# A two-layer trunk on one core: input loads moved in the queue, maxima taken one by one inside blocks, fewer gate products kept for the end, and output weights loaded before they are split

## The chip, the cores and the metric

The kernel runs on one core of a Trainium2 chip. The metric is the device time of one execution in microseconds (us). A core has five engines, each with an instruction stream of its own, that meet over semaphores: TensorE (PE in the profile; PEld is its weight load), VectorE (DVE), ScalarE (ACT), GpSimd (POOL) and SyncE (SP), which here only issues DMAs.

## The reference

The sequence has 2048 tokens, the model width is 1024, all in float32, and the result has to keep float32 accuracy. Layer 0 is forgetting attention with 16 heads of 64; layer 1 is sliding-window attention (window 128) with 16 query heads over 4 shared heads, and learned sinks.

```
u = rmsnorm(x, norm_a_g);  q, k, v, f, gate = split(u @ w_in_a)
q, k = rmsnorm per head(q), rmsnorm per head(k)
c = cumsum(log_sigmoid(f + b_forget))                      # per head, over the tokens
p = softmax(q.k / 8 + c[query] - c[key], causal);  o = p @ v
h = x + (o * silu(gate)) @ w_out_a
k_s, v_s = split(rmsnorm(h, kv_norm_g) @ w_kv)             # 4 heads; k normed, rotated
q, gate = split(rmsnorm(h, norm_b_g) @ w_in_b)             # 16 heads; q normed, rotated
o = softmax over the last 128 keys and the head's sink (q.k / 8) @ v_s
out = h + (o * silu(gate)) @ w_out_b
```

## The kernel before, in words

Every float32 product of the projections is made as three products of split operands: a tile is cast to a rounded half (the names with h: `uh`, `wh`) and a remainder (`ul`, `wl`), and uh·wh, uh·wl and ul·wh are summed. So a block of 128 tokens by 512 columns over the depth of 1024 (8 slices of 128, index `dt`) is 24 matmuls, at L571.

The stages follow each other in this order.

1. **Projections of layer A** (`projections`). Seven groups of columns (v of heads 0 to 7, two of k, three of q, the middle one of which waits for the forget logits of the one ahead of it, then v of heads 8 to 15), each over 16 token blocks `tb`. In the first group the token tiles are loaded as they are needed: `norm` loads one x tile of 128x1024 (L298), ACT squares it (L300), L286 to L291 make the factor, L304 scales; `norm_transpose` turns it on PE (L277) and splits it (L313 on ACT, L314 on DVE). `normer.upto` keeps two tiles loaded ahead. The small vectors (gains, biases, sinks; `load_vectors`, L212) and the positions (L228) are loaded on the same SP queue; `vectors` and `angles` use them at blocks VECTORS_AT and ANGLES_AT. `weights` loads raw weights (L337, two slices of `dt` in one DMA), and ACT and DVE split them (L350 and L351, with a gain L354 and L355).
2. **The forget gates** (`forget`): the jobs of that function, among them `running` (matmuls at L614 with a triangle and a matrix of ones, DVE at L619 and on) and `rows` (transposes and rows written out), run at the blocks FORGET_AT of the next group.
3. **Maxima ahead.** The attention (`attention_a`) is a generator. In the last v group `hook(tb)` calls it: it starts with `load_max` for head 0 (L680 to L682: ka, ca, qa in forms for the maxima) and then `max_pieces`, one for each 128 queries and up to 1024 keys: matmuls (L738) into a PSUM tile `b2`, and DVE's running maximum (L747, L752). EARLY of them run there; at piece REST_AT `load_rest(0)` loads what the scores of head 0 need (L686, L687, L693). During projections PSUM has three tiles `b2`, which the blocks and the pieces share, and `pa`, `pb`.
4. **Attention A**: 320 steps, each a 128-key-block pair of `scores` (L784, L785; exponent on ACT L793, cast L798, remainder on POOL L799, sums on DVE L810) and `values` (L825, three steps later), with maxima of later heads (`ahead`) and `gate`, a filler that yields one product at a time (768 in all, L855: weights `wr` loaded from `wg` at L851, results stored at L862). `feed((total - KEPT) * (n + 1) // 320)` spreads all products but KEPT over the steps; eight each follow the last three steps. At the steps PREP_AT one pair of heads is finished (`gated_load`, L986 to L991, then `gated`: POOL L1001, DVE L1004 and L1005, ACT L1006, DVE L1007).
5. **The tail of attention A.** The last sums are inverted (`recips`, L709), the rest of the filler runs, and between its products `half` loads and splits the first half of w_out_a (tile `st`), calling `between(k)` after each two slices for the pairs that are left. Then `out_a` loads and splits the second half in the same way (L337, `st`), multiplies (L1045) and adds x.
6. **Layer B**: projections of shared k and v, of q and gate, then `attention_b`, units of 128 tokens and one shared head, with the output projection (L1191) as its filler. At unit B_AHEAD the first half of w_out_b, `W[0]`, is loaded and split (four loads of `wr`, L337; ACT L350, DVE L351).

The order on each engine is set by the framework's scheduler, which takes instructions as they become ready by priority; `keep_in_program_order` pins an instruction behind the one written before it on its engine. Tiles are buffers of named slots that are passed on when their last reader is done: `big` 8, `st` 4, `wr` 2, `wh` and `wl` 9 each, `qn` 3, `sq` 2. All DMAs are issued by SP in one order, and one that waits holds those behind it.

Of the kernel before, what the change touches and what calls it, by code (L numbers as in the profile page):

```python
# [21 lines left out]
P = 128  # L22
# [8 lines left out]
CH = 512  # L31
# [12 lines left out]
PREP_AT = (286, 294, 304, 311)  # L44
# [3 lines left out]
KEPT = 6 * 3 * NDT  # L48

NORM_AHEAD = 2  # L50
QK_LAG = 1
# [4 lines left out]
EARLY = 21  # L56
REST_AT = 8

VECTORS_AT = 11
ANGLES_AT = 9  # L60
FORGET_AT = (1, 3, 5, 6, 7, 8)
# [23 lines left out]
class Trunk:  # L85
# [124 lines left out]
    def load_vectors(self, loads):  # L210
        for t, src in loads:
            self.nc.sync.dma_start(out=t, in_=src, allow_slow_non_contiguous=True)  # L212
# [10 lines left out]
    def angles(self):  # L223

        nc, a = self.nc, self.a
        sh = [P, NTB, 8]
        pi = self.sb("sq", [P, NTB], I32)
        nc.sync.dma_start(  # L228
            out=pi, in_=a["positions"].rearrange("(t p) -> p t", p=P),
            allow_slow_non_contiguous=True,  # L230
        )
# [44 lines left out]
    def flip(self, out, in_):  # L276
        self.nc.tensor.transpose(out, in_, self.ident)  # L277
# [38 lines left out]
    def weights(  # L316
        self, src, c0, w, gain=None, extra=None, into=None, ahead=None, tag="wr", between=None
    ):

# [11 lines left out]
        for dt in range(NDT):  # L331
# [94 lines left out]
    def normer(self, src):  # L426
# [11 lines left out]
        def upto(n, loads=()):  # L438

            loads = list(loads)  # L440
# [12 lines left out]
    def projections(self, normed, groups, later=None, pre=None, hook=None):  # L453
# [8 lines left out]
        if pre is not None:  # L462
# [11 lines left out]
            norm(1, [partial(load_raw, 0), partial(self.load_vectors, self.loads[:1])])  # L474
            for dt in range(2, NDT, 2):
                load_raw(dt)
# [48 lines left out]
        for gi, grp in enumerate(groups):  # L525
# [31 lines left out]
            for tb in range(NTB):  # L557
                norm(tb + NORM_AHEAD)
                if hook is not None and gi == len(groups) - 1:
                    hook(tb)  # L560
# [8 lines left out]
                for dt in range(NDT):  # L569
                    for i, (u, k) in enumerate(((uh, 0), (uh, 1), (ul, 0))):  # L570
# [28 lines left out]
    def forget(self, z):  # L599
# [10 lines left out]
        def running():  # L610
            both = self.ps("b2", [P, 2, NTB, H])
            inb, tot = both[:, 0], both[:, 1]
            for o, m in ((inb, self.tri), (tot, self.ones)):
                nc.tensor.matmul(  # L614
                    o.rearrange("p t h -> p (t h)"), m, flat, start=True, stop=True
# [6 lines left out]
        def rows(ch):  # L622
            sc = -float(HD) ** 0.5
            tr = self.ps(("pa", "pb")[ch % 2], [H, 4, P])
            for j in range(4):
                self.flip(tr[:, j, :], z[:, ch * 4 + j, :])
# [27 lines left out]
    def attention_a(self, w_out, result):  # L654
# [64 lines left out]
        def max_pieces(h, ch):  # L719
# [5 lines left out]
            def piece(j, part):  # L725
# [11 lines left out]
                for b in range(nb):  # L737
                    nc.tensor.matmul(  # L738
# [3 lines left out]
                    )  # L742
                o = m[:, j : j + 1] if parts == 1 else mt[:, j, part : part + 1]
# [154 lines left out]
        def prepare_load():  # L898
# [4 lines left out]
            if k < 5 or k % 2 == 0:  # L903
# [29 lines left out]
        for n, (u, p) in enumerate(steps):  # L933
# [17 lines left out]
            if n == SILU_AT:  # L951
                silus()
            if n in PREP_AT:
# [20 lines left out]
    def half(self, w, i, tag="wr", between=None):  # L974
# [3 lines left out]
            w, i * CH, CH, tag=tag, between=between,  # L978
# [77 lines left out]
    def attention_b(self, w_out, res, dst):  # L1056
# [152 lines left out]
        for n in range(N + V_LAG_B):  # L1209
# [6 lines left out]
            if n == B_AHEAD:  # L1216
                W[0] = self.weights(w_out, 0, CH)
# [18 lines left out]
    def layer_a(self):  # L1236
# [27 lines left out]
        def hook(tb):  # L1264
            if tb >= MAX_AT:
                next(steps)
# [82 lines left out]
```

## Time and profile before

| | before |
|---|---|
| time, median of 3 runs | 2584.24 us (2583.28 to 2587.08) |
| time of the profiled execution | 2575.79 us |
| its span | 2574.1 us, TensorE clock granted 0.991 on average |
| PE busy | 2488.1 us, 97 % |
| DVE, ACT, POOL busy | 1671.7, 1357.1, 939.4 us |
| DMA | 420.34 MB, 163 GB/s on average |

The span runs from the first to the last instruction of the profiled execution, and all positions below are microseconds from its start. A wait is listed with the engine that stood, the instruction that stood (tile, line), and what it waited for. "2.0, 1, 2.0" behind it is the sum, how often, and the longest. A row of the timeline has the start, the length, the engine, line, operation, the tile written and read, and in brackets how long the engine had been idle and for what.

### The profile page before, as it was taken

Reading aid. Unit: us, or ns where it says so; the run is one execution under the profiler, and the core shown is the slowest. Engines: PE = TensorE matmul, PEld = TensorE weight load, DVE = VectorE, ACT = ScalarE, POOL = GpSimd, SP = SyncE. Lnnn points to the kernel's source line nnn. Section 1 sums busy time; section 2 is a strip of 40 time slices with the busy share of each in tenths; the row PEclk is TensorE's granted clock in tenths of the full one; section 3 lists DMA queues with packets and bytes.
Section 4 is the critical chain, followed back from the end, with each engine's and each line's share of the span. In section 5 each row is a group of like instructions: output and inputs, shape, how many; then the busy total and the mean of one; then the engine's idle time right before and its main releaser. Section 6 shows DMA issues by size and latency. Waiting matters only on the chain. (4 is left out here: it accounts for less than half of the span.)

```text
span 2574.1 us, 37683 instructions
## 1 busy us (share of the span) xinstructions
PE 2488.1 (97%) x12414; PEld 2069.8 (80%) x12414; DVE 1671.7 (65%) x4125; ACT 1357.1 (53%) x2645; POOL 939.4 (36%) x611
## 2 busy tenths in 40 slices
PE   7999999989999999999999979999999999899999
PEld 6888899967888777787787758778888888788887
DVE  5455556623888878888888834446756401688885
ACT  5423323312878788787788732224422213777774
POOL 0000000010878777888778822200011000355552
PEclk9999999999999999999999999999999999999999
DMA  5556555676654665566554678964434513756642
GB/s 165 172 171 177 163 149 163 188 216 197 169 151 121 189 168 184 149 179 187 135 145 136 175 224 246 272 207 140 138 96 115 152 70 117 207 147 170 172 140 66
DMA packets 357298, 420.34 MB, mean 163 GB/s; under 512 B 65104, under 2 KB 248400, under 8 KB 350928
## 3 DMA queue, kind: packets, MB, share of 16 engines
q1 hardware_dynamic: 357104, 417.94, 56.1%
q8 instruction: 98, 1.61, 0.3%
q14 instruction: 96, 0.79, 0.1%
HBM read 264.23 MB, written 153.49 MB: 162 GB/s over the span
## 5 line engine op out<-in xcount | busy, mean ns | idle before, releaser
L571 PE MATMUL b<-wh,big 128*128 128x512 f32 (+3 forms) x2560 | 771.7, 376 | 11.1 <-DVE mt L747 4.3
L799 POOL TENSOR_TENSOR big<-st,big 128x1024 fp32r<-128x1024 f32 (+1 forms) x320 | 678.7, 2134 | 255.5 <-ACT big L798 199.3
L571 PEld LDWEIGHTS b<-wh,big 128*128 128x128 f32 x2560 | 472.6, 189 | 85.2 <-DVE mt L747 6.3
L571 PE MATMUL b<-wl,big 128*128 128x512 f32 (+3 forms) x1280 | 474.4, 371 | 0.3 <-DVE wl L355 0.3
L810 DVE TENSOR_TENSOR ac<-ac,st 128x512 f32<-128x512 f32 (+3 forms) x576 | 355.4, 617 | 60.9 <-ACT st L793 32.3
L825 PE MATMUL pa<-big 128*128 128x512 f32 (+2 forms) x1280 | 329.3, 372 | 1.6 <-POOL big L799 0.8
L793 ACT ACTIVATE st<-sc 128x512 f32<-128x512 f32 (+1 forms) x512 | 274.3, 585 | 100.5 <-PE sc L785 61.7
L798 ACT CAST big<-st 128x1024 fp32r<-128x1024 f32 (+1 forms) x320 | 302.6, 946 | 7.8
L571 PEld LDWEIGHTS b<-wl,big 128*128 128x128 f32 x1280 | 242.3, 189 | 36.0 <-DVE wl L355 2.6
L825 PEld LDWEIGHTS pa<-big 128*128 128x128 f32 x1280 | 224.8, 190 | 41.8 <-ACT sq L833 6.4
L784 PE MATMUL sc<-big 128*128 128x512 f32 (+2 forms) x640 | 245.9, 384 | 3.0 <-ACT st L793 3.0
L367 ACT ACTIVATE sq<-b 128x512 f32<-128x512 f32 (+2 forms) x128 | 66.2, 517 | 339.5 <-PE b L571 339.4
L747 DVE CUSTOM_DVE_ANT_0 mx<-mx,rot 128x960 f32<-128x960 f32 (+3 forms) x242 | 213.1, 880 | 47.5 <-PE mx L738 43.9
L785 PE MATMUL sc<-big 67*128 67x512 f32 (+2 forms) x640 | 235.7, 368 | 0.0
L855 PE MATMUL pb<-wh,wr 128*128 128x512 f32 x512 | 189.9, 407 | 19.5 <-DMA wr<-wg 18.4
L738 PE MATMUL mx<-big 66*128 66x320 f32 (+2 forms) x666 | 194.9, 365 | 5.2 <-DVE mt L752 2.9
L369 DVE TENSOR_REDUCE sm<-sq 128x8 f32<-128x512 f32 (+2 forms) x128 | 74.9, 585 | 172.0 <-ACT sq L367 171.8
L1045 PE MATMUL b<-big 128*128 128x512 f32 x768 | 178.6, 393 | 5.6 <-DVE qn L1049 4.3
L1045 PEld LDWEIGHTS b<-big 128*128 128x128 f32 x768 | 144.8, 190 | 38.5 <-DVE qn L1049 5.7
L542 PE MATMUL b<-big,wh 128*128 128x512 f32 x512 | 158.6, 391 | 0.9 <-ACT st L548 0.9
L664 POOL MEMSET rot<- 128x1024 bf16 x1 | 1.0, 951 | 428.7 <-PE pb L277 428.7
L1126 POOL TENSOR_TENSOR st<-st,rs 128x1024 f32<-128x1024 f32 (+1 forms) x64 | 118.5, 1852 | 98.8 <-DVE rs L1125 89.7
(212 smaller groups left out, 4193.5 us busy)
## 6 DMA issues: line engine op xcount, KB each, us to landing
wr<-wg SPq DMA_DIRECT2D x64, 512.0 KB
va<-st SPq DMA_DIRECT2D x32, 512.0 KB
ka<-st SPq DMA_DIRECT2D x64, 256.0 KB
ut<-big SPq DMA_DIRECT2D x16, 1024.0 KB
big<-ka SPq DMA_DIRECT2D x16, 1024.0 KB
big<-qa SPq DMA_DIRECT2D x16, 1024.0 KB
qb<-st SPq DMA_DIRECT2D x64, 256.0 KB
big<-qb SPq DMA_DIRECT2D x16, 1024.0 KB
```

Of the source, the lines that this page charges most:

```text
L571: nc.tensor.matmul(ps[:, :n], u[tb // 4][:, dt, us], W[k][dt], start=(dt == 0 and i == 0), stop=(dt == NDT - 1 and i == 2),)
L738: nc.tensor.matmul(ps[:, b, :wb], qb[:66, i * P : (i + 1) * P], kb[:66, k0 + b * wb : k0 + (b + 1) * wb], start=True, stop=True,)
L747: nc.vector.tensor_tensor_reduce(out=lg, in0=lg, in1=mask, scale=1.0, scalar=NEG, op0=ALU.add, op1=ALU.max, accum_out=f_(o),)
L784: nc.tensor.matmul(o, ka[:, ks], qa[:, qs], start=not (last and n_), stop=False)
L785: nc.tensor.matmul(o, kb[:, ks], qb[:, qs], start=False, stop=not diag)
L793: nc.scalar.activation(pf[:, off : off + w], ps[:, :w], AF.Exp, scale=HD**-0.5)
L798: nc.scalar.copy(ph[:, :tw], pf[:, :tw])
L799: nc.gpsimd.tensor_tensor(pl[:, :tw], pf[:, :tw], f_(ph[:, :tw]), ALU.subtract)
L810: nc.vector.tensor_tensor(a_, a_, pf[:, off : off + w], ALU.add)
L825: nc.tensor.matmul(pv[:, q0 : q0 + w], v[:, k, :], src[:, off : off + w], start=(p == 0 and n_ == 0 and i == 0), stop=(last and n_ == 1 an ...
L855: nc.tensor.matmul(ps, w[:, dt // 2 % 2, wk, dt % 2, :], us[dt][uk], start=(dt == 0 and i == 0), stop=(dt == NDT - 1 and i == 2),)
L1045: nc.tensor.matmul(ps, y[p // 4][:, k, p % 4, ts_], W[nh][j][p], start=(p == 0 and i == 0), stop=(p == NDT - 1 and i == 2),)
```

## The change: eight edits

- **Start.** The loads of the vectors and of the positions are pinned in program order, VECTORS_AT goes from 11 to 8 and ANGLES_AT from 9 to 11, `upto` loads three tiles ahead, and the raw weights of the first group are asked for behind x tile 1 in one piece.
- **Forget gates.** FORGET_AT is spread to later blocks, and the matmuls of `running` and the transposes of `rows` are pinned.
- **Maxima.** `hook` is called for every `dt`: `load_max` stays at block 5, and from block 8 on one piece goes behind the products of dt 0, 3 and 5 of each block, in place of two pieces at the start of each block from 5 on. EARLY is 24 (all of head 0) in place of 21, REST_AT 3 in place of 8, and the pieces' matmuls are pinned.
- **Gate products.** KEPT is 96 in place of 144.
- **Output weights of layer A.** At step 302 the raw first half of w_out_a is loaded in four DMAs into one `big` tile; `half` splits them from that tile. The second half is loaded through `st` as before.
- **Pairs.** PREP_AT has five steps in place of four, so a fifth pair of heads is finished within the steps; the tiles of pair 5 and 7 are `qn`, `wh`, `wl` in place of `st`.
- **`between`** feeds in every call.
- **Output weights of layer B.** `W[0]` is made in four parts, at units 6 to 9, two slices each.

```diff
-PREP_AT = (286, 294, 304, 311)
+PREP_AT = (284, 293, 304, 309, 314)
+RAW_AT = 302
-KEPT = 6 * 3 * NDT
+KEPT = 4 * 3 * NDT
+LOADED_AHEAD = 3
-EARLY = 21
-REST_AT = 8
-VECTORS_AT = 11
-ANGLES_AT = 9
-FORGET_AT = (1, 3, 5, 6, 7, 8)
+EARLY = 24
+REST_AT = 3
+VECTORS_AT = 8
+ANGLES_AT = 11
+FORGET_AT = (1, 5, 8, 9, 10, 11)
...
 def load_vectors(self, loads):
     for t, src in loads:
-        self.nc.sync.dma_start(out=t, in_=src, allow_slow_non_contiguous=True)
+        self.tc.keep_in_program_order(
+            self.nc.sync.dma_start(out=t, in_=src, allow_slow_non_contiguous=True)
+        )
...
 def weights(self, src, c0, w, ..., between=None,
+    dts=range(NDT),
...
-        for dt in range(NDT):
+        for dt in dts:
...
 def upto(n, loads=()):
-                while done[0] < min(done[1] + 2, NTB):
+                while done[0] < min(done[1] + LOADED_AHEAD, NTB):
                     ready.append(self.norm(src, done[0], junk))
                     done[0] += 1
-                    if loads:
-                        loads.pop(0)()
+                    if done[0] > 1:
+                        for load in loads:
+                            load()
+                        loads = ()
...
             for tb in range(NTB):
                 norm(tb + NORM_AHEAD)
-                if hook is not None and gi == len(groups) - 1:
-                    hook(tb)
...
                 for dt in range(NDT):
+                    if hook is not None and gi == len(groups) - 1:
+                        hook(tb, dt)
                     for i, (u, k) in enumerate(((uh, 0), (uh, 1), (ul, 0))):
...
-        yield
         for n in range(EARLY):
+            yield
             if n == REST_AT:
                 load_rest(0)
             ahead(n + 1)
-            yield
+        yield
...
-            if k < 5 or k % 2 == 0:
+            if k != 6:
                 tiles = [self.sb(t, [P, CH]) for t in ("qn", "wh", "qn", "wl")]
...
             feed((total - KEPT) * (n + 1) // len(steps))
+            if n == RAW_AT:
+                raw = self.sb("big", [P, NDT, CH])
+                for dt in range(0, NDT, 2):
+                    nc.sync.dma_start(out=raw[:, dt : dt + 2, :], in_=w_out[...])
...
         def between(k):
-            prepare()
-            if k < 3:
+            if prepared < NDT:
+                prepare()
+            if len(ready) < NDT:
                 prepare_load()
-                feed(fed + (total - fed) // (4 - k))
+            feed(fed + (total - fed) // (4 - k))
-        result.append(self.half(w_out, 0, "st", between))
+        result.append(self.half(w_out, 0, ahead=raw, between=between))
...
-            if n == B_AHEAD:
-                W[0] = self.weights(w_out, 0, CH)
+            if B_AHEAD <= n < B_AHEAD + NDT // 2:
+                hs, ls = self.weights(w_out, 0, CH, dts=(2 * (n - B_AHEAD), 2 * (n - B_AHEAD) + 1))
+                W[0] = [W[0][0] + hs, W[0][1] + ls] if W[0] else [hs, ls]
...
-        def hook(tb):
-            if tb >= MAX_AT:
-                next(steps)
+        def hook(tb, dt):
+            if (tb, dt) == (MAX_AT, 0) or tb >= MAX_AT + 3 and dt in (1, 4, 6):
                 next(steps)
```

The order of SP at the start, before. `st<-in_x` and `wr<-in_x` are the token tiles, `big<-in_w_in_a` the first weights, the short tiles the small vectors:

```order
L467 DMA big<-in_w_in_a 128x2x512 x4
L298 DMA st<-in_x 128x1024
L298 DMA wr<-in_x 128x1024 x2
L228 DMA sq<-in_positions 128x16x1
L212 DMA bf<-in_b_forget 128x16
L212 DMA g_qa<-in_qnorm_a_g 64x1 x2
L212 DMA g_ka<-in_knorm_a_g 64x1 x2
L212 DMA g_b<-in_norm_b_g 128x8x1
L212 DMA g_kv<-in_kv_norm_g 128x8x1
L414 DMA va<-st 128x8x128
L212 DMA g_qb<-in_qnorm_b_g 64x1 x2
```

The same place after:

```order
L478 DMA big<-in_w_in_a 128x2x512 x4
L306 DMA st<-in_x 128x1024
L306 DMA wr<-in_x 128x1024 x2
L306 DMA st<-in_x 128x1024
L424 DMA va<-st 128x8x128
L306 DMA wr<-in_x 128x1024
L424 DMA va<-st 128x8x128
L306 DMA st<-in_x 128x1024
L424 DMA va<-st 128x8x128
```

The positions and the vectors stood ahead of the x tile of block 4 and the first store of v; now the x tiles go on, the vectors come between the va stores of blocks 5 to 7 (five and nine of them, behind the x tiles of blocks 9 and 10), and the positions behind the store of block 10.

PE at the first maxima, in the last v group, before (L571 is the block, L738 a piece; the number tells the PSUM tile):

```order
L571 MATMUL b_5245<-wh,big 128x512
L738 MATMUL b_5290<-big 128x128
L571 MATMUL b_5293<-wh,big 128x512
...
L571 MATMUL b_5293<-wh,big 128x512
L738 MATMUL b_5322<-big 128x256
L738 MATMUL b_5325<-big 128x384
L571 MATMUL b_5329<-wh,big 128x512
```

And after, where a block is at L584 and a piece at L753:

```order
L753 MATMUL b_5382<-big 128x128
L584 MATMUL b_5377<-wh,big 128x512
...
L584 MATMUL b_5377<-wh,big 128x512
L753 MATMUL b_5394<-big 128x256
L584 MATMUL b_5377<-wh,big 128x512
...
L584 MATMUL b_5377<-wh,big 128x512
L753 MATMUL b_5403<-big 128x384
L584 MATMUL b_5377<-wh,big 128x512
```

Two pieces between two blocks became one piece each between products of one block, and the first piece comes three blocks later.

SP behind the last store of inverted sums (`rd`), before. `wr<-wg` are weights of the filler, `gt` its results, `om`, `oc`, `rd` what a pair needs:

```order
L715 DMA rd<-sq 48x32
L851 DMA wr<-wg 128x1024 x2
L862 DMA gt<-sq 128x512
L337 DMA st<-in_w_out_a 128x2x512 x2
L986 DMA st<-om 128x512
L987 DMA st<-oc 128x512
L851 DMA wr<-wg 128x1024
L988 DMA st<-gt 128x512
L851 DMA wr<-wg 128x1024
L862 DMA gt<-sq 128x512
L991 DMA st<-rd 64x512 x2
```

After:

```order
L730 DMA rd<-sq 48x32
L1013 DMA qn<-gt 128x512
L879 DMA gt<-sq 128x512
L347 DMA st<-in_w_out_a 128x2x512
L868 DMA wr<-wg 128x1024
L347 DMA st<-in_w_out_a 128x2x512
L868 DMA wr<-wg 128x1024
L879 DMA gt<-sq 128x512
L347 DMA st<-in_w_out_a 128x2x512
L868 DMA wr<-wg 128x1024
```

Until the pairs that come last are loaded, four weights of the filler and four pairs of slices of w_out_a (the second half) are behind that store now, where there were ten and seven (of both halves).

More of the change, by code (lines that the diff above doesn't have):

```diff
@@ L276, in flip @@
     def flip(self, out, in_):
-        self.nc.tensor.transpose(out, in_, self.ident)
+        return self.nc.tensor.transpose(out, in_, self.ident)
     def rstd(self, sm, n, count):
@@ L316, in weights @@
     def weights(
-        self, src, c0, w, gain=None, extra=None, into=None, ahead=None, tag="wr", between=None
+        self, src, c0, w, gain=None, extra=None, into=None, ahead=None, tag="wr", between=None,
+        dts=range(NDT),
     ):
@@ L472, in load_raw @@
                 )
-            norm(1, [partial(load_raw, 0), partial(self.load_vectors, self.loads[:1])])
-            for dt in range(2, NDT, 2):
-                load_raw(dt)
+            norm(
+                1,
+                [partial(self.load_vectors, self.loads[:1])]
+                + [partial(load_raw, dt) for dt in range(0, NDT, 2)],
+            )
         else:
@@ L613, in running @@
             for o, m in ((inb, self.tri), (tot, self.ones)):
-                nc.tensor.matmul(
-                    o.rearrange("p t h -> p (t h)"), m, flat, start=True, stop=True
+                self.tc.keep_in_program_order(
+                    nc.tensor.matmul(
+                        o.rearrange("p t h -> p (t h)"), m, flat, start=True, stop=True
+                    )
                 )
@@ L737, in piece @@
                 for b in range(nb):
[L738 removed]
+                    mm = nc.tensor.matmul(
                         ps[:, b, :wb], qb[:66, i * P : (i + 1) * P],
@@ L742, in piece @@
                     )
+                    if "mx" not in self.banks:
+                        self.tc.keep_in_program_order(mm)
                 o = m[:, j : j + 1] if parts == 1 else mt[:, j, part : part + 1]
@@ L952, in attention_a @@
                 silus()
+            if n == RAW_AT:
+                raw = self.sb("big", [P, NDT, CH])
+                for dt in range(0, NDT, 2):
+                    nc.sync.dma_start(
+                        out=raw[:, dt : dt + 2, :],
+                        in_=w_out[dt * P : (dt + 2) * P, :CH].rearrange("(k p) c -> p k c", p=P),
+                    )
             if n in PREP_AT:
```

15 lines of the change are left out of this document (8 added, 7 removed).

## The prediction

> **What bounds the kernel now.** I read the page's busy times first, then PE's waits, then the timeline at each long wait. The page says that PE is the bound:
>
> ```profile
> PE 2488.1 (97%) x12414; PEld 2069.8 (80%) x12414; DVE 1671.7 (65%) x4125; ACT 1357.1 (53%) x2645; POOL 939.4 (36%) x611
> ```
>
> Of the span of 2574.1 us PE is idle for 86. By the order of the two programs each engine has the same instructions after the change, so only this idle time, and time at a lower PE clock, can be won. The view of waits of PE, longest first (some left out):
>
> ```profile
> PE pb L855 <- DMA wr<-wg: 18.4, 14, 4.8
> ...
> PE b L738 <- DMA big<-qa: 7.8, 1, 7.8
> PE b L277 <- DVE sm L289: 5.7, 1, 5.7
> PE b L1097 <- DVE wl L351: 5.4, 1, 5.4
> ...
> PE b L571 <- DVE mt L747: 4.3, 6, 0.8
> ...
> PE sc L784 <- ACT st L793: 3.0, 1, 3.0
> ...
> PE b L571 <- DVE m L747: 2.8, 4, 1.1
> ...
> PE b L571 <- DVE st L619: 2.0, 1, 2.0
> ```
>
> Each row but the sixth is one that an edit aims at; the sixth is a price that an edit could raise. I go through them in the order of the program.
>
> **Start.** The timeline of SP (start, length, operation; first and last of the small loads), then ACT, PE, and two windows (their columns: length, busy time of PE, PEld, DVE, ACT, POOL with counts, PE clock, DMA share, GB/s):
>
> ```profile
> 12.07 0.43 SPq L228 DMA_DIRECT2D sq<-in_positions  x1
> ...
> 26.76 0.43 SPq L212 DMA_DIRECT2D gk<-in_knorm_b_g  x1
> 27.24 0.43 SPq L298 DMA_DIRECT2D st<-in_x  x1
> 33.33 1.06 ACT L300 ACTIVATE big<-st 128x1024 fp32r<-128x1024 f32 x1 [4.25 <-DMA st<-in_x]
> 39.23 1.94 PE L277 MATMUL b<-ident,st 128*128 128x128 f32 x8 [5.71 <-DVE sm L289]
> 35.00:40.00 5.00, 0.77 (x4) 0.80 (x5) 2.91 (x12) 2.58 (x6) 0.00 (x0) 0.88 0.19 64
> 40.00:45.00 5.00, 5.00 (x21) 4.22 (x20) 1.55 (x2) 1.01 (x1) 0.00 (x0) 0.78 0.53 163
> ```
>
> The small loads hold SP from 12.07 to 27.2; the x tile of block 4 is issued only then, lands at 33.3, and PE stands 5.71 us, then runs a slice of 5 us at clock 0.78, which is 1.1 us more. With the x tiles ahead of the small loads both go: 5.7 + 1.1, about 7. In exchange SP meets the small loads at blocks 5 to 7, behind the x tile of block 9. A matmul of a block takes 0.23 us (21 of them in the 4.80 us between two rows of the next fence, 562.16 and 566.96), so the 24 of a block take 5.5, and nothing of block 9 is due before five blocks, 27 us, have passed since tile 4; the issuing of all the small loads took 15. I take 7, with 4 (the queue is late once more) and 7.7 as ends.
>
> **Forget gates.** `running` with its DVE part now has two more blocks to become ready, 11 us for a wait of 2.0 (last row of the waits). I take 2, ends 0 and 2.3.
>
> **Maxima.** SP, then PE, the window of the first block behind a piece, and the page's group of DVE's maxima (busy time, mean ns of one):
>
> ```profile
> 547.25 0.53 SPq L682 DMA_DIRECT2D big<-qa  x1
> 553.21 0.45 PE L738 MATMUL b<-big 66*128 66x128 f32 x1 [7.81 <-DMA big<-qa]
> 560.96 0.46 PE L738 MATMUL b<-big 66*128 66x256 f32 x2
> 561.82 0.50 PE L571 MATMUL b<-wh,big 128*128 128x512 f32 x1 [0.41 <-DVE m L747]
> 562.16 0.40 PE L571 MATMUL b<-wl,big 128*128 128x512 f32 x1
> 566.96 0.39 PE L571 MATMUL b<-wl,big 128*128 128x512 f32 x1
> 553.46:560.96 7.50, 7.50 (x26) 6.02 (x26) 0.36 (x2) 0.00 (x0) 0.00 (x0) 0.72 0.41 90
> L747 DVE CUSTOM_DVE_ANT_0 mx<-mx,rot 128x960 f32<-128x960 f32 (+3 forms) x242 | 213.1, 880 | 47.5 <-PE mx L738 43.9
> ```
>
> The first piece follows the issue of qa by 6 us and PE pays 7.81 for it; the block behind it takes 7.50 us at clock 0.72, 2 more than 5.5. Then each pair of pieces holds two of three `b2` tiles, and the next block waits until DVE has given one back: the two rows with L747 in the waits, 4.3 + 2.8 = 7.1 in ten waits. All together 16.9. After the change three blocks, over 16 us, lie between the loads and the first piece, against the 14 (6 + 7.8) that they took. A piece comes every 7 to 10 matmuls, 1.6 to 2.3 us, and DVE takes 0.88 for one, with 0.7 for the block's own remainder: a bank is back before the next is asked for. DVE does 3 x 0.88 + 0.7 = 3.3 us in some 7. So nothing should be left; I take 15.5 and leave 1.4 for a remnant. The three pieces that now run here are not run in the attention, which makes no difference to PE. Ends: 8 (the waits for DVE stay, and qa is late by 2) and 16.9. `load_rest(0)` goes ahead of the rows of m on SP, and no reader needs it sooner.
>
> **Tail of attention A.** From the last inversion of sums to the first product of out_a, as one window; two slices of it; its waits for `wg`; two of these in the timeline; then the 63 us before it, and the attention from 960 on:
>
> ```profile
> 1499.47:1550.60 51.13, 35.45 (x124) 26.20 (x124) 13.65 (x21) 12.08 (x22) 2.76 (x2) 0.87 0.82 253
> 1505.00:1510.00 5.00, 5.00 (x13) 3.85 (x13) 1.34 (x3) 1.83 (x4) 0.00 (x0) 0.50 0.98 370
> 1525.00:1530.00 5.00, 3.15 (x8) 2.50 (x9) 1.21 (x2) 1.14 (x2) 0.00 (x0) 0.70 0.90 332
> PE pb L855 <- DMA wr<-wg: 15.0, 8, 4.8
> 1504.57 0.77 PE L855 MATMUL pb<-wh,wr 128*128 128x512 f32 x1 [4.82 <-DMA wr<-wg]
> 1526.85 0.65 PE L855 MATMUL pb<-wh,wr 128*128 128x512 f32 x1 [2.17 <-DMA wr<-wg]
> 1436.00:1499.00 63.00, 58.30 (x275) 44.72 (x274) 52.64 (x77) 45.72 (x73) 51.48 (x25) 1.00 0.51 138
> 960.00:1500.00 540.00, 529.22 (x2568) 421.62 (x2566) 456.07 (x814) 423.99 (x659) 430.18 (x205) 0.99 0.57 162
> ```
>
> 120 products stand here (144 kept less the 24 fed behind the last three steps): 27.6 us at 0.23. The other 23.5 are 15.0 of waits for `wg`, (1 - 0.87) x 51.1 = 6.6 at a low clock, and 2 of small things. The bound is DMA: share 0.82, 253 GB/s, which over 51.13 us is 12.9 MB: ten `wg` and seven w_out_a loads of 0.52 MB, and the rest gates and pairs.
>
> After, 72 products remain (96 less 24), 16.6 us. Six `wg`, three w_out_a loads and half of the pair's loads, some 6 MB, go to the 63 us before, where the share is 0.51; near 6 MB stay, at 253 GB/s 24 us, at the best slice's 370 16 us. I take 21 for the stage, between 16.6 (PE) and 25. The 48 products move into the steps, where PE has no room: 11.1 us there. So 51 - 21 - 11 = 19, ends 23.4 and 15.
>
> The steps themselves get heavier. POOL there:
>
> ```profile
> 1460.89 1.56 POOL L1001 TENSOR_TENSOR qn<-qn,wh 128x512 f32<-128x512 f32 x1 [0.78 <-PE sc L785]
> ...
> 1478.90 15.67 POOL L799 TENSOR_TENSOR big<-st,big 128x1024 fp32r<-128x1024 f32 x7 [3.09 <-ACT big L798]
> ```
>
> POOL needs 2.2 us for a step's remainder and is busy nearly throughout; the fifth pair adds one L1001 of 1.5 us and moves others later, with four to five DVE operations. The one wait of PE there is the sixth row of the waits, 3.0. I take 2.5 off, between 0 and 8 (each of three L1001 and its pair's DVE work passed on in full). The pinned queue: the raw load at step 302 waits on SP for a free `big`, and `wg` loads stand behind it; the ends above hold it up to 3 us. Net here 16.5, ends 4 and 23.4.
>
> The Trainium skill, page TensorE: Matmul & The Clock Gate, section HAM oscillation, asks for a PE gap of more than about 3.4 us before the clock falls. Of the trace the 4.82 agrees (0.50 behind it); the slice with 0.70 follows waits that were each shorter, the longest 2.17, so here the row decides. By the page a tail with only short waits would keep the full clock and my 21 would be 1 or 2 less.
>
> **Layer B.** SP and a window:
>
> ```profile
> 2209.82 0.39 SPq L337 DMA_DIRECT2D wr<-in_w_out_b  x1
> ...
> 2219.44 0.46 SPq L1074 DMA_DIRECT2D big<-kb  x1
> ...
> 2225.25 0.37 SPq L337 DMA_DIRECT2D wr<-in_w_out_b  x1
> 2219.00:2235.00 16.00, 9.76 (x50) 8.13 (x49) 12.50 (x38) 11.63 (x30) 6.30 (x5) 0.89 1.01 298
> ```
>
> Four loads of 0.52 MB come on a full DMA (share 1.01), and ACT and DVE split eight slices in a row; PE stands 5.4 and then runs at 0.89 on average, 1.8 us more. Spread over four units the loads of the next kb go ahead. But bytes and splits are the same, `wr` has two buffers, and the last pair now ends closer to its first use at unit 8 or later. I take 4, ends -3 and 7.2.
>
> LOADED_AHEAD also acts at layer B's first tiles, and `between` feeds once more; I find no wait there of over 1 us and take 0 (ends -2 and 1).
>
> **Sum.** 7 + 2 + 15.5 + 16.5 + 4 = 45. The profiled execution took 2575.79, so 2530.8 in its terms; it lies 8.4 us below the median of 2584.24, on which the measurement rests: 2539.
>
> **The rivals.**
> - *The tail stays with DMA.* What leaves it only makes the steps' loads late: share 0.57 there, but SP is one queue, and `wr` has two buffers. For it: the 18.4 of the first row contains 3.4 outside the tail. If the stage takes 30 us, the gain there is 10 less 2.5, and the time 2548.
> - *The last steps pay.* POOL and DVE are passed on in full and more, 10 us in place of 2.5, or the fifth pair's loads hold SP: 2547 to 2555. For it speaks POOL at 51.48 of 63 us; against it that DVE and ACT have 10 to 17 us of room there.
> - *Pieces still wait.* Pieces within a block hold two of three tiles while the block holds one; if each block begins with a wait of 0.7 (as the rows of L747 have) at eight blocks, and qa is still late, place three gives 8 and the time is 2547.
> - *PE is the tail's bound.* The slice at 370 GB/s shows what passes when many loads are open; at that rate 6 MB take 16.2 us, under PE's 16.6, so the gain there is 23.4 in place of 19 and the time 2535. The Trainium skill, page DMA: Bandwidth & Descriptors, section Bandwidth, puts a core's HBM limit near 358 GB/s, which speaks for this; the stage's mean of 253 speaks against it.
> - *Slower.* The raw load at step 302 waits on SP for its `big` tile, with `wg`, `om` and `rd` behind it. PE executes in order, so a filler product without weights stops the scores too. The price is a us for each us of blocking. It decides at 45 us, which is 17 steps of 2.6 us (205 operations of POOL, about one a step, in the 540 us), of the 18 that are left. A single load of 0.52 MB that must wait for one attention tile is a matter of a few steps, so this is unlikely: 2585 to 2595.
>
> **How the numbers follow.** Chances: my sum 0.49, PE-bound tail 0.10, DMA tail 0.13, last steps 0.12, pieces 0.08, slower 0.04, no net effect because several of these meet 0.04. The likeliest is 2539, with its own range of 2526 to 2556 from the ends (all the upper ones give 58; all the lower ones give 11, and I go half of the way there, since they have causes of their own). The range for 8 in 10 takes in the rivals, and two of them together (9 + 8 + 8 off: 2564): 2520 to 2566. Under 0.2 %, 5 us, no difference can be told from none (the runs before spread over 3.8 us). Faster by more: all cases but the last two, 0.92; within: 0.04; slower: 0.04.
>
> **What would show it.** In the changed profile: no wait of L277 near 39 us; the piece at block 8 without a wait for qa, and no L747 in PE's waits for blocks; from the last inversion to out_a about 21 us at a clock above 0.9; an idle time of PE near 50 in place of 86; in layer B the wait for L351 gone. I am wrong if waits for `wr<-wg` keep over 10 us, if PE waits for L793 or POOL grow past 8 in the last 20 steps, or if a new wait of PE for a `va` store, a vector or `ca` appears where the queue was reordered.

## The result and the profile after

The changed kernel takes 2555.83 us in the median (2549.98 to 2558.07, four runs), the kernel before 2584.46 in the same comparison: a ratio of 0.9884, interval 0.9866 to 0.9903, so 28.6 us less. The forecast was 2539 and 45 us less, the range 2520 to 2566. The profiled execution took 2549.98 us, 25.8 below the one of before. First the page's busy times, then PE's waits (some left out):

```profile
PE 2486.3 (98%) x12414; PEld 2070.7 (81%) x12414; DVE 1681.5 (66%) x4125; ACT 1360.4 (53%) x2645; POOL 941.2 (37%) x611
```

```profile
...
PE b L584 <- ACT wh L364: 6.8, 3, 4.7
PE pb L872 <- DMA wr<-wg: 4.6, 6, 2.1
PE sc L801 <- ACT st L810: 4.0, 1, 4.0
PE b L584 <- DVE big L322: 3.6, 2, 2.6
PE mx L753 <- DVE mt L764: 3.6, 2, 2.7
PE pb L872 <- ACT sq L878: 3.4, 1, 3.4
...
PE b L1122 <- DMA big<-kb: 2.5, 1, 2.5
PE pa L1181 <- DVE wr L1190: 2.2, 2, 1.5
PE pa L285 <- DVE qn L393: 1.9, 3, 1.3
...
PE b L1122 <- DVE big L1170: 1.4, 1, 1.4
```

PE is idle for 61.9 us in place of 86.0. Of the eight rows that the prediction showed, six are gone (qa, the x tile, `wl` of layer B, the two of L747 at the blocks, and L619), `wg` fell from 18.4 to 4.6, and the feared one, PE's wait for the exponent (L793, now L810), rose from 3.0 to 4.0. But six rows here stand for waits that the kernel before did not have, or had under 1.3 us (ACT wh, DVE big L322, ACT sq, kb, qn L393, L1170).

Both programs have the same 12414 PE records, so the same matmul can be found in both timelines. This table has the starts of such matmuls, and what the stage between them gained:

| up to | before | after | gained in all | in this stage | forecast |
|---|---|---|---|---|---|
| block 4 of the first v group | 47.84 | 40.57 | 7.3 | 7.3 | 7 |
| end of the group in which the forget gates run | 466.39 | 455.35 | 11.0 | 3.8 | 2 |
| first scores of attention A | 632.02 | 604.38 | 27.6 | 16.6 | 15.5 |
| matmul of the last inversion of sums | 1499.54 | 1483.00 | 16.5 | -11.1 | -11 - 2.5 |
| first product of out_a | 1550.60 | 1512.07 | 38.5 | 22.0 | 30 |
| last product of out_a | 1736.59 | 1694.55 | 42.0 | 3.5 | 0 |
| matmul 96 of layer B's first group | 1761.63 | 1735.86 | 25.8 | -16.3 | 0 |
| first scores of layer B | 2172.58 | 2147.14 | 25.4 | -0.3 | 0 |
| scores of unit 16 | 2275.08 | 2249.53 | 25.6 | 0.1 | 4 |

At the last product of out_a the change was 42 us ahead. Then the start of layer B took 16 back: PE stood 10.0 us in that stage, and the granted clock was 0.88 over its 41.3 us. The SP timeline at that place, after (L306 loads an h tile, L1075 stores one, L347 loads w_kv), the first and last of the ACT splits, and PE's last transposes of out_a and first product of layer B:

```profile
1672.93 0.37 SPq L306 DMA_DIRECT2D wr<-h  x1
...
1683.92 12.10 SPq L1075 DMA_DIRECT2D h<-qn  x3
1696.12 17.93 SPq L347 DMA_DIRECT2D wr<-in_w_kv  x4
1699.79 1.34 ACT L364 ACTIVATE wh<-wr,g_kv 128x512 fp32r<-128x512 f32 x2 [2.92 <-DMA wr<-in_w_kv]
...
1717.22 1.33 ACT L364 ACTIVATE wh<-wr,g_kv 128x512 fp32r<-128x512 f32 x2 [4.40 <-DMA wr<-in_w_kv]
1694.78 1.03 PE L285 MATMUL b<-ident,wr 128*128 128x128 f32 x8
1700.57 0.80 PE L584 MATMUL b<-wh,big 128*128 128x512 f32 x1 [4.75 <-ACT wh L364]
```

The first and last of the four w_kv loads before:

```profile
1714.98 0.38 SPq L337 DMA_DIRECT2D wr<-in_w_kv  x1
...
1733.29 0.38 SPq L337 DMA_DIRECT2D wr<-in_w_kv  x1
```

Before, all four were issued ahead of the end of out_a (1736.6). After, the sixth tile of h, loaded ahead at 1672.93, holds one of the two `wr` buffers, and the other is given back only by the transposes at 1694.78. So the weights pass one by one through a single buffer, 5.9 us each, all behind the end of out_a, and PE waits, runs at half clock (0.52 granted from 1700 to 1705), and waits again.

The tail of attention A took 29.07 us, not 21. The window of the stage, two slices of it, PE's waits in the timeline, and what DVE and ACT did at the first of them (rows left out between):

```profile
1483.00:1512.07 29.07, 21.65 (x74) 16.48 (x75) 10.02 (x16) 7.45 (x13) 0.00 (x0) 0.82 0.78 236
1485.00:1490.00 5.00, 3.37 (x8) 2.72 (x9) 1.98 (x4) 1.10 (x2) 0.00 (x0) 0.51 0.79 241
1505.00:1510.00 5.00, 5.00 (x15) 3.94 (x16) 1.29 (x2) 1.14 (x2) 0.00 (x0) 0.66 0.84 219
1486.63 0.80 PE L872 MATMUL pb<-wh,wr 128*128 128x512 f32 x1 [3.43 <-ACT sq L878]
1496.37 0.47 PE L872 MATMUL pb<-wh,wr 128*128 128x512 f32 x1 [1.53 <-DMA wr<-wg]
1499.70 0.50 PE L872 MATMUL pb<-wh,wr 128*128 128x512 f32 x1 [0.32 <-DMA wr<-wg]
1504.90 0.47 PE L872 MATMUL pb<-wh,wr 128*128 128x512 f32 x1 [2.15 <-DMA wr<-wg]
1480.42 3.69 DVE L361 TENSOR_TENSOR big<-big 128x512 fp32r<-128x512 f32 x6
1484.04 0.68 DVE L1029 TENSOR_TENSOR st<-st 128x512 f32<-128x512 f32 x1
1485.48 0.62 ACT L1031 CAST big<-st 128x512 fp32r<-128x512 f32 x1 [3.69 <-DVE st L1030]
1486.00 0.58 ACT L878 COPY sq<-pb 128x512 f32<-128x512 f32 x1
DMA to landing us min/median/max: 4.1/4.5/5.1
```

Read from below: PE can't go on before ACT has copied the finished gate tile (L878); ACT stands at the pair's cast ahead of it (L1031); that waits for DVE, and DVE first did six remainders of w_out_a (L361), ready so early because the raw weights had come early. But the order of cast and copy is not new. The kernel before has it too, with no remainder ahead of the pair:

```profile
1501.71 0.62 ACT L1006 CAST big<-st 128x512 fp32r<-128x512 f32 x1 [3.38 <-DVE st L1005]
1502.23 0.58 ACT L861 COPY sq<-pb 128x512 f32<-128x512 f32 x1
```

There the copy ended at 1502.81, 3.1 us after PE had stopped at 1499.75; with the change it ended 3.4 us after. Before, it did not show as a wait, because PE stood until 1504.57 for `wg` in any case (the 4.82 in the prediction). The change took the longer wait away, and the one under it came to light. (The pair is the one with index 6: its tiles go to `st` with the change, which the list of edits does not say.)

In the fence ahead of this one, the last row is the time from issue to landing of the `wg` loads here. The stage is 16.6 us of products, 7.4 of waits and (1 - 0.82) x 29.07 = 5.2 of low clock. The two slices show again that the clock falls behind a wait of 3.43, and also behind one of 2.15.

In layer B's attention the split weights took away the wait of 5.4, and these came, in the window from 2183 to 2252 us (the scores of unit 16 start at 2249.53):

```profile
PE b L1122 <- DMA big<-kb: 2.5, 1, 2.5
PE pa L1181 <- DVE wr L1190: 2.2, 2, 1.5
PE b L1122 <- DVE big L1170: 1.4, 1, 1.4
PE b L285 <- POOL st L1151: 1.3, 1, 1.3
PE pb L1216 <- DVE wl L361: 0.9, 1, 0.9
PE b L285 <- DVE mx L1132: 0.3, 1, 0.3
```

They are 8.6 us, for 9.3 before (5.4, 2.5 and 1.4). The loads and splits of this place are the same, and PE waits for them here or there.

### The profile page after: what moved, and what is told of

Its sections match the earlier page's. It is cut to its first block, busy times and chain, and to the rows that moved or that the text cites. A ratio compares the mean times of both kernels' runs of the same rounds, so it can differ in the third digit from the quotient of the medians.

```text
span 2548.2 us, 37618 instructions
## 1 busy us (share of the span) xinstructions
PE 2486.3 (98%) x12414; PEld 2070.7 (81%) x12414; DVE 1681.5 (66%) x4125; ACT 1360.4 (53%) x2645; POOL 941.2 (37%) x611
## 4 chain that ended last, share of the span: by engine, by line
PE 84%; DMA 7%; DVE 4%; issue 2%; ACT 2%; SPq 1%; POOL 0%; DVEq 0%; ACTq 0%; POOLq 0%
PE b L584 29%; PE pa L842 10%; PE b L555 7%; PE pb L872 6%; PE pb L1216 6%; PE sc L801 5%; PE sc L802 5%; PE mx L753 5%; PE b L285 3%; PE pa L1181 2%; DMA wr<-rd 1%; PE b L1070 1%; PE b L1125 1%; PE b L1122 1%; PE pa L285 1%
## 5 line engine op out<-in xcount | busy, mean ns | idle before, releaser
L584 PE MATMUL b<-wh,big 128*128 128x512 f32 (+3 forms) x2560 | 775.0, 377 | 10.5 <-ACT wh L364 6.8
L584 PEld LDWEIGHTS b<-wh,big 128*128 128x128 f32 x2560 | 473.8, 189 | 81.7 <-ACT wh L364 8.9
L584 PE MATMUL b<-wl,big 128*128 128x512 f32 (+3 forms) x1280 | 476.3, 373 | 0.1
L810 ACT ACTIVATE st<-sc 128x512 f32<-128x512 f32 (+1 forms) x512 | 275.4, 585 | 101.9 <-PE sc L802 67.2
L584 PEld LDWEIGHTS b<-wl,big 128*128 128x128 f32 x1280 | 243.2, 190 | 37.6 <-DVE wl L365 4.5
L764 DVE CUSTOM_DVE_ANT_0 mx<-mx,rot 128x128 f32<-128x128 f32 (+3 forms) x240 | 211.0, 879 | 47.8 <-PE mx L753 45.7
L753 PE MATMUL mx<-big 66*128 66x128 f32 (+3 forms) x660 | 192.7, 365 | 6.1 <-DVE mt L764 3.6
```

The costliest lines, as they stand in the source:

```text
L584: nc.tensor.matmul(ps[:, :n], u[tb // 4][:, dt, us], W[k][dt], start=(dt == 0 and i == 0), stop=(dt == NDT - 1 and i == 2),)
L753: mm = nc.tensor.matmul(ps[:, b, :wb], qb[:66, i * P : (i + 1) * P], kb[:66, k0 + b * wb : k0 + (b + 1) * wb], start=True, stop=True,)
L810: nc.scalar.activation(pf[:, off : off + w], ps[:, :w], AF.Exp, scale=HD**-0.5)
```

## The experiments

Ratios are to the kernel before, measured in the same comparison. The twelve experiments come from four comparisons, in which the kernel before took 2581.39 to 2585.65 us; so differences of a few us between experiments are read from the stages in their profiles, beside the times.

**1 and 2. The tiles loaded ahead in layer B.** In the changed kernel, taken back for layer B alone (the function around L306 gets the number as an argument):

```diff
-def normer(self, src):
+def normer(self, src, ahead=2):
-    while done[0] < min(done[1] + LOADED_AHEAD, NTB):
+    while done[0] < min(done[1] + ahead, NTB):
-    self.normer(x), groups, ...
+    self.normer(x, LOADED_AHEAD), groups, ...
```

> The changed kernel, with three tiles loaded ahead only in layer A's first group and two, as before the change, in layer B. Theory: the sixth tile of h takes a `wr` buffer ahead of the four loads of w_kv, so these pass one by one through the other buffer, and PE loses 16.6 us at the start of layer B. Then this gives 16 us back (14 to 17), about 2539 in the median and 2533 where the changed kernel's profile had 2548, with the w_kv loads issued before the end of out_a and no wait of the first block for wh. Rival: the loads are late because the stores of h hold SP (12 us in the trace) in the faster kernel; then less than 5 us comes back.

2539.00 us, ratio 0.9832 (0.9815 to 0.9849), and these loads:

```profile
1676.87 0.38 SPq L347 DMA_DIRECT2D wr<-in_w_kv  x1
...
1696.88 0.38 SPq L347 DMA_DIRECT2D wr<-in_w_kv  x1
```

They are all issued before out_a ends (1698.48), and PE has no wait in the first group of layer B. The converse, three tiles ahead in layer B of the kernel before (`min(done[1] + ahead, NTB)` with 3 for h alone):

> The kernel before the change, with three tiles of h loaded ahead in layer B alone. Theory: this one edit costs what layer B's start lost, 12 to 17 us: about 2598 in the median. Rival (the loss comes from the rest of the change, which brings out_a to another state): under 3 us.

2598.44 us, ratio 1.0064 (1.0046 to 1.0082), 17 us slower. In the profiles the stage from the last product of out_a to matmul 96 of layer B takes 25.0 us in all ten kernels of this study with two tiles ahead there, and 41.3 to 42.7 in the four with three (the changed kernel and experiments 2, 3 and 4). So from both sides this one number costs 16 to 17 us, and the rest of the change has no part in it.

**3. Output weights of layer B in one piece.**

```diff
-if B_AHEAD <= n < B_AHEAD + NDT // 2:
-    hs, ls = self.weights(w_out, 0, CH, dts=...)
-    ...
+if n == B_AHEAD:
+    W[0] = self.weights(w_out, 0, CH)
```

> The changed kernel, with the first half of w_out_b loaded and split in one piece at unit 6, as before. Theory: the split only exchanged one wait of 5.4 us for five smaller ones, the time stays within 2 us of the changed kernel (2554 to 2558). Rival, the prediction's term: 4 us slower.

2554.94 us, ratio 0.9900 (0.9878 to 0.9922). From the first scores to unit 16 it took 102.8 us, the changed kernel 102.4. Its waits there, from 2187 to 2257 us:

```profile
PE b L1122 <- DVE wl L361: 5.4, 1, 5.4
PE pa L1181 <- DVE wr L1190: 1.9, 2, 1.7
PE pb L1216 <- DVE sq L1221: 1.5, 1, 1.5
```

The split gave nothing that can be told: this stage takes 101.6 to 106.3 us in the eleven kernels with the split and 102.5 to 102.8 in the three without it (the kernel before, experiments 2 and 3). The prediction's 4 us were an exchange of one wait for others.

**4. Remainders of the raw weights pinned.**

```diff
-nc.vector.tensor_tensor(lo, raw, f_(h), ALU.subtract)
+op = nc.vector.tensor_tensor(lo, raw, f_(h), ALU.subtract)
+if ahead is not None:
+    self.tc.keep_in_program_order(op)
```

> The changed kernel, with the remainders of the w_out_a slices that come from the raw tile pinned in program order on DVE, so that only two and not eight of them run ahead of the sixth pair. Theory: in the tail of attention A the eight early remainders hold DVE, DVE holds ACT's cast of the pair, and this holds the copy that PE waits for 3.43 us, with half a clock behind it; pinned, the wait falls under 1 us and the tail takes 23 to 25 us in place of 29: 4 to 6 us faster. Rival: the tail is bound by its DMA (236 GB/s over it), and the time moves by less than 2 us.

2553.35 us, ratio 0.9890 (0.9873 to 0.9907), which can't be told from the changed kernel's; the tail took 27.5 us, 1.6 less, and the wait for the copy was 2.7 in place of 3.4, far from the expected fall under 1. DVE's remainders were no longer last there:

```profile
1481.79 0.69 DVE L1031 TENSOR_TENSOR st<-st 128x512 f32<-128x512 f32 x1 [1.99 <-DMA st<-rd]
1484.41 0.58 ACT L880 COPY sq<-pb 128x512 f32<-128x512 f32 x1 [0.56 <-DMA oc<-sq]
```

Now the pair's load of `rd` and the copy's own buffer came last. So the remainders were 0.7 us of the wait; the rest is the pair's own loads, and the copy's place behind its cast.

**5. The second half of w_out_a out of the tail**, on the kernel of experiment 1: `W = [first, ([], [])]`, and two slices of the second half made at each of the first four blocks of out_a.

> The kernel of the first experiment (two tiles ahead in layer B, 2539), with the four loads of the second half of w_out_a taken out of the tail of attention A and put between the first four blocks of out_a, where their bytes are used 22 us later. Theory: the tail is bound by DMA (6.9 MB at 236 GB/s in 29 us), so without 2.1 of these MB it takes 20 to 23 us in place of 29 to 30; out_a has few idle us and a DMA share near 0.9, and may give back up to that much: 2531 to 2540 in all. Rival: the tail is bound by the chain of pairs, the copy of the gate tile and the two `wr` buffers, then it stays within 2 us of 29.

2539.24 us, ratio 0.9829 (0.9804 to 0.9854). The tail did not shrink but took 33.1 us, as neither expectation had it, and as a test of bytes this failed: SP filled the free `st` buffers with the loads of the next pairs, so 223 GB/s over 33.1 us are 7.4 MB, where experiment 1 had 7.05. It tells only that the edit as such wins nothing.

**6 and 7. KEPT 48 and KEPT 144**, on the kernel of experiment 1 (`KEPT = 2 * 3 * NDT`, `6 * 3 * NDT`).

> The kernel of the first experiment, with KEPT 48 in place of 96: 48 more gate products go from the tail into the steps, where they cost PE 11.1 us. Theory (tail bound by DMA, a product there costs its weights' bytes, 0.065 MB or 0.27 us at 240 GB/s, hardly more than its 0.23 on PE): the tail shrinks by 11 to 14 us, and the total stays within 3 us of 2539. Rival, the prediction's way of counting (each product moved away saves the tail its wait too): 4 to 8 us faster.

> The kernel of the first experiment, with KEPT 144 as before the change, the raw load and the five pairs staying. Theory: as for KEPT 48, the gain of the tail comes from the bytes of w_out_a and the pair that were moved, not from the products; the tail grows by 11 to 14 us, the steps shrink by 11.1, and the total stays within 3 us of 2539. Rival: it loses 6 to 10 us, because the products were what the tail waited with.

2534.25 us, ratio 0.9805 (0.9783 to 0.9826), and 2543.83, ratio 0.9847 (0.9818 to 0.9876), beside 2539.00 with 96. Per 48 products the tail changes by 17.0 (30.0 to 13.0) and 13.1 us (43.1 to 30.0), and the steps of the attention by 13.3 and 13.6 us. So a product costs 0.28 us in the steps, not 0.23, and 0.27 to 0.35 in the tail. With KEPT 48 the median came out as the rival had it, 4.8 us faster; with KEPT 144 the tail and the steps cancel to 0.5 us, as the theory had it, and the 4.8 us lost lie in out_a, which took 6.8 longer. (The expectation's 0.065 MB for a product is a slip: a load of 0.52 MB serves 12 products, which is 0.044.) The tail with KEPT 144:

```profile
1472.14:1515.21 43.07, 31.35 (x123) 23.28 (x123) 8.24 (x13) 8.73 (x15) 3.87 (x3) 0.96 0.85 260
```

The same 120 products took 51.1 us before, so the raw load, the fifth pair and the new `between` made it 8 us less together: PE's idle time fell from 15.7 to 11.7 us and the loss to a low clock from 6.6 to about 1.7. Which of the three did it was not tried.

**8. The maxima as before**, on the kernel of experiment 1:

```diff
-EARLY = 24
-REST_AT = 3
+EARLY = 21
+REST_AT = 8
...
-if "mx" not in self.banks:
-    self.tc.keep_in_program_order(mm)
...
-if (tb, dt) == (MAX_AT, 0) or tb >= MAX_AT + 3 and dt in (1, 4, 6):
+if tb >= MAX_AT and dt == 0:
+    next(steps)
     next(steps)
```

> The kernel of the first experiment, with the maxima as before the change (two pieces at the start of each block from block 5 on, 21 of them, the rest of head 0 loaded at piece 8, no pins). Theory: the ten waits for DVE, the wait for qa and the slow block behind it come back, 16.6 us: 2553 to 2557. Rival: a part of the gain came from elsewhere (the loads in another order), then under 10 us.

2558.41 us, ratio 0.9897 (0.9875 to 0.9920): 17 us slower than experiment 1 by the ratios and 19 by the medians, and in the profile the stage up to the first scores is 18.0 us longer, with the waits of before back one by one:

```profile
PE b L753 <- DMA big<-qa: 8.5, 1, 8.5
PE b L584 <- DVE mt L762: 4.3, 6, 0.8
PE b L584 <- DVE m L762: 2.8, 4, 1.1
```

**9. KEPT 48 with the remainders pinned** (6 and 4 together).

> The kernel with KEPT 48 and two tiles ahead in layer B (2534), with the remainders of the raw slices pinned as in the fourth experiment. Theory: with 24 products left, the tail of 13.0 us is 5.5 of products, the one wait of 5.71 for the copy behind the pair's cast, and a low clock behind it; with two in place of eight remainders ahead of the pair the wait falls to 3.5 to 5, and the time by 1 to 3 us: 2531 to 2533. Rival: the pair's own loads set that wait, under 0.5 us.

2534.36 us, ratio 0.9805 (0.9778 to 0.9832). The wait for the copy fell from 5.71 to 3.2 and the tail from 13.0 to 10.6 us, as the theory had it, but the time did not follow: the 2.4 us are below what the runs can tell (2531.9 to 2538.6), and out_a lost 1.4 of them in its profile (PE for the `qn` tile, 4.9 us in place of 3.4).

**10. No early raw load**, on the kernel of experiment 1: the four loads at step 302 left out, and `half(w_out, 0, "st", between=between)`.

> The kernel of the first experiment (2539), with the first half of w_out_a loaded in the tail through `st`, as before the change; KEPT 96 and the five pairs stay. Theory: the tail is bound by its bytes, and 2.1 MB at 235 to 253 GB/s make it 8 to 9 us longer, less the 2 to 3 us that the early remainders cost: 5 to 8 us slower, 2544 to 2547. Rival: the wait for the copy and the half clock behind it are the tail's main loss, so without early remainders the time stays within 2 us.

2533.87 us, ratio 0.9801 (0.9773 to 0.9830). My theory fell. Three of the four loads, 1.6 MB, are back inside the tail, and it took 28.4 us, not 38. Its window, then DVE at the pair and PE's first wait:

```profile
1482.24:1510.68 28.44, 20.80 (x75) 15.50 (x75) 10.27 (x16) 9.64 (x17) 1.26 (x1) 0.88 0.87 293
1483.99 0.69 DVE L1022 TENSOR_TENSOR st<-st 128x512 f32<-128x512 f32 x1 [1.15 <-DMA st<-rd]
1486.59 0.75 PE L872 MATMUL pb<-wh,wr 128*128 128x512 f32 x1 [4.15 <-ACT sq L878]
```

293 GB/s where experiment 1 had 235 on the same stage: the tail was not full of bytes. The Trainium skill, page DMA: Bandwidth & Descriptors, section Bandwidth, with its limit near 358 GB/s for a core, agrees that there was room; the slice of 370 GB/s in the kernel before lies above that figure.

The wait for the copy is there without any early remainder, and longer, 4.15 us; the pair's own load of `rd` came last ahead of DVE. So early remainders did not bring this wait. Most of what the profile gained on experiment 1 lies in out_a, 176.6 us for 183.2, without a wait for `qn`; it is the fastest of the four runs (2528.23), and why out_a went better was not tried. The early raw load, one part of the change, gave nothing that the runs show.

**11. The start as before**, on the kernel of experiment 1 (pins, VECTORS_AT, ANGLES_AT and the tiles ahead in layer A).

> The kernel of the first experiment, with the loads of the vectors and positions, and the number of x tiles ahead, as before the change. Theory: the wait of 5.7 us for the x tile of block 4 and the half clock behind it come back, 7.3 us: 2545 to 2548. Rival: the queue's later order hides a part, under 4 us.

2548.36 us (2539.75 to 2550.10), ratio 0.9849 (0.9822 to 0.9875): 9 us slower than experiment 1 by the medians, 4 by the ratios. In its profile block 4 of the first group stands 8.5 us later, and 8.2 of it stay until the second group. This profile is of the fastest run, though, and later stages gave back all but 0.3 us of it; so the step is shown at its place, and what it is worth in the whole time is known only to some us.

**12. A third buffer for the filler's weights in the tail**, on the kernel of experiment 1:

```diff
-w = self.sb("wr", [P, 2, 2, 2, P], F32R)
+load = (ch * NDT + ft) * 2 + dt // 4
+w = self.sb("st" if load in (57, 60, 63) else "wr", [P, 2, 2, 2, P], F32R)
```

> The kernel of the first experiment (2539), with every third of the last loads of the filler's weights put into a tile `st` in place of `wr`, so that three and not two are in flight in the tail. Theory, formed after the seventh and tenth experiments: the tail is paced by the landing of these loads (4.1 to 5.1 us from issue, through two buffers, for 12 products of 2.8 us), not by bytes; with a third buffer the waits for wg in the tail (1.2, 0.4, 1.9 and 1.0 in the profile of the first experiment) fall under 1.5 us together, the tail from 30.0 to 25 to 27 us, and the time by 3 to 5 us: 2534 to 2536. The wait of 3.7 for the copy stays. Rival: bytes set the pace, the waits stay within 1 us of 4.5 and the tail above 29.

2532.97 us (2531.50 to 2534.10), ratio 0.9803 (0.9780 to 0.9827), and the tail 25.3 us. Its waits, first here, then those of experiment 1 in the same stage:

```profile
PE pb L873 <- ACT sq L879: 4.6, 2, 3.9
PE pb L873 <- DMA wr<-wg: 0.9, 1, 0.9
```

```profile
PE pb L872 <- DMA wr<-wg: 4.5, 4, 1.9
PE pb L872 <- ACT sq L878: 3.7, 1, 3.7
```

This is what the theory of landings asked for. A load serves 12 products, 2.8 us of PE; it lands 4.5 us after its issue and is issued when a buffer comes free, so with two buffers each load makes PE wait some 1.7 us (the waits reach 2.1), and with three it need not. More bytes beside it did not make this worse: experiment 10 has 3.5 us of these waits at 293 GB/s, experiment 1 has 4.5 at 235. (The stage moved 232 GB/s, so 5.9 MB for 7.05, since the third buffer is one of `st`; that fewer bytes shortened it is argued against by experiment 10 and not by a run of its own.) The wait for the copy stayed, as expected. Of the kernels tried, this one, 6, 9 and 10 are the fastest, 50 us below the kernel before; their intervals overlap, and their edits were not all put together.

## Why the prediction was right, and where it was wrong

The time lies in the range and the direction is right, but 28.6 us came of 45, and the likeliest course was not the one that happened. Experiment 1 hits 2539 because the misses that are left cancel. Of the signs that the prediction named, an idle time near 50 us (61.9) and a clock above 0.9 in the tail (0.82) did not come; nor did any of those that would have shown it wrong.

- **Start**: 7 forecast, 7.3 in the trace, 8.5 at the same place when undone (experiment 11). The step held, the cover too: no wait appeared where the small loads went.
- **Forget gates**: 2 forecast, 3.8 measured, above its end of 2.3. The two waits (2.0 and 0.3) are gone; where the other 1.5 came from was not tried.
- **Maxima**: 15.5 forecast, 16.6 at the first scores, 18.0 in that stage when undone (experiment 8). The mechanism was right in all its parts: qa has landed, and no block waits for a bank.
- **The 48 products in the steps**: 11.1 forecast by 0.231 us each, 11.1 in the trace of the change, but 13.3 to 13.6 by experiments 6 and 7. That the trace agrees is luck: the three pieces that now run ahead took six matmuls out of the steps, and PE was idle there for 11.6 us against 13.7. So the 2.5 for heavier last steps did not show as a sum: PE's waits near the end grew from 6.2 to 8.4 us, and there was less before it.
- **Tail**: the step that was mis-sized. 21 us were forecast, 29.07 came, which was the rival "the tail stays with DMA" by its price (30 us) but not by its cause. I set the bound as bytes at 253 GB/s; experiment 10 shows that more bytes took no longer, and experiment 12 that the number of buffers against the landing time sets the waits for `wg`. The sum of bytes had slips of its own. 12.9 MB less 6 are 6.9, not near 6 (the stage moved 6.9), so its own rate gave 27 us; and I took six `wg` loads off, where 48 products need four, and in the timeline ten became five. Last, I counted the waits for `wg` as if nothing lay under them. Under the 4.82 lay 3.1 us for the copy behind the pair's cast; it came out as 3.4, with half a clock behind it. The early remainders were 0.7 us of this wait (experiment 4), and with KEPT 48 they were 2.5 (experiment 9); without them it is there all the same (experiment 10).
- **The clock**: by the Trainium skill, page TensorE: Matmul & The Clock Gate, section HAM oscillation, only a gap above some 3.4 us would have been followed by a low clock. The 3.43 agrees; the slice at 0.66 behind 2.15 does not; and experiment 7, with 11.7 us of waits in its tail, none over 2.33, kept 0.96 over these 43 us. So short waits cost clock in one of these places and not in the other, and the row was the safer guide.
- **LOADED_AHEAD in layer B**: taken as 0, ends -2 and 1; it cost 16.3 to 17 us. This is the largest miss: a term put at nothing. It lay in the order of the two programs: the sixth `wr<-h` stands ahead of the four w_kv loads there. I had looked for a wait of PE in the kernel before and not at whose buffer the extra tile takes.
- **Layer B's attention**: 4 forecast, 0.1 measured, nothing by experiment 3. I named the reason against it (the same bytes and splits) and did not weigh it.
- **out_a**: 0 forecast, 3.5 gained, with PE's waits for L1074 2.8 us in place of 4.3 and the rest at a slightly higher clock (1.00 for 0.99); the stage takes 176.6 to 189.9 us in the kernels of this study, and why was not tried.

The rival on the other side, the raw load blocking SP at step 302, did not happen: SP stood 2.2 us at that load, and no wait of PE came of it.

## What to carry to other kernels

When an edit loads one tile more ahead, ask which buffer that tile takes and what stands behind it in the queue for the same buffers; on a shared pool of two, one tile more ahead left four weight loads a single buffer, behind the end of the stage before, and cost 17 us in a stage the edit was not written for. When PE waits for a stream of loads, compare the landing time with the work that a load feeds, times the buffers less one, before calling it a matter of bandwidth. And before a long wait is priced as a gain, look at what else would have held the engine until then: here 4.8 us of waiting for weights covered 3.1 us of waiting for a copy, and taking the first away left the second.

## What the runs showed of the hardware

The same stage of 72 products moved 223 to 293 GB/s from one kernel to the next, with `wg` loads of 0.5 MB landing in 4.1 to 5.9 us in each profile where that could be read. A product that is spread over the attention's steps, where PE is 98 % busy, cost 0.28 us, against 0.23 in a dense run of blocks.
